# Attention keys turned with both parts at once, subtractions moved from GpSimd to VectorE, and modulation sums cut into other chunks

## The chip, the cores and the metric

One core of a Trainium2 chip runs the whole program. The metric is device microseconds from launch to end. The core has TensorE (matmuls, PE), VectorE (DVE), ScalarE (ACT), GpSimd (POOL) and SyncE (SP), which here only issues DMAs; GpSimd and ScalarE issue some too. Each engine runs its own instructions in the order fixed when the program was built.

## The reference, cut to what matters

Two layers over 512 latent and 256 context tokens of width 1024, in float32. Layer 0 has the Fourier and convolution mixer, layer 1 windowed attention with 16 query heads on 4 key heads of width 64. Every layer takes shift, scale and gate vectors from a modulation `silu(c) @ w_mod[layer] + b_mod[layer]` (six vectors of 1024), and ends in a mixture of experts behind a router:

```python
mod_l = (jax.nn.silu(c) @ w_mod[layer] + b_mod[layer])[:, None, :]
sh1_l, sc1_l, g1_l, sh2_l, sc2_l, g2_l = jnp.split(mod_l, 6, axis=-1)
hl = modulate(rms_norm(xl, norm_mix_g[layer]), sh1_l, sc1_l)
...
xl = xl + g1_l * yl
hl2 = modulate(rms_norm(xl, norm_ffn_g[layer]), sh2_l, sc2_l)
f = hier_moe(hl2, ...)     # router logits: hl2 @ w_router; 32 experts, top 2 of one group
```

In the attention, a score is the product of a normed and rotated query with a normed and rotated key, each 64 wide.

## The kernel before

Work is done in tiles of 128 tokens: `m` = 0 to 3 latent, 4 and 5 context. A float32 product that must be exact enough is made of two parts: an upper part `hi` (rounded to the type fp32r) and a lower part `lo = x - hi`, with three or four products of parts in place of one.

**The first mixer (lines 1200 to 1365, the functions `proj`, `four_a`, `four_b`).** Four Fourier groups `g` are followed by four convolution chunks `j`; each chunk makes three projections `proj` (48 matmuls each, L1259 and L1260), for which ScalarE writes `whi` (L1253) and VectorE `wlo` (L1255). Between them two other jobs are fed in small steps. `ModFeed.step` (`feed`) makes the modulation of layer 0 and the first third of layer 1's by matmuls (L1037) on 2 MB pieces of `w_mod`. `SumFeed.step` (`sums`) makes vectors 2 to 5 of layer 1's modulation on VectorE: 4 vectors of 8 steps, each step a multiply and add of a 128x1024 tile `mw` into `acc` (L1075). The tiles `mw`, 512 KB each, are loaded by DMAs that GpSimd issues (L1068); there are two buffers, and a load is issued when the step before last has left its buffer. After a vector's eighth step `finish` sums `acc` over the partitions by four matmuls (L1088), adds the bias on VectorE (L1090), and stores the vector to the DRAM table `mod_d` (L1091). The 32 steps lie three to a Fourier group (12) and five to a chunk (20); the last is at the very end of the last chunk.

**Where the sums lie in memory.** `acc` and `mw` are in the pool `sp`, which stands on the right-hand side beside `hp` (48 KB per partition, the mixer's inputs `hhi` and `hlo`). When the chunks are done, `cp, tp, sp, hp` are closed and the same place is given to `lst`, `x1p` (24 KB), `hq` (20 KB) and `rq`. In the program before, the tiles of `rq`, which are the router's weights `wr`, biases `br`, gains `gf`, the gate row `gr` and the router's modulation `md`, lie over `acc` and `mw`: `wr`, `br`, `gf` and the first `gr` over `acc`, `md` over a buffer of `mw`. A tile's load waits for the last user of the tiles under it.

**`mixer_out` (from line 1368).** It multiplies the mixer's output `ym` by `w_out` in two halves of the columns: per token tile 24 matmuls (L1436) into one of two PSUM tiles `A`, then VectorE multiplies by `gr` (L1440) and adds into `x1` (L1441). After the first tiles, `router` loads `md` (L1383) and makes 8 accumulated float32 matmuls on it, 16 in the trace (L1389). SyncE issues all of these loads. Then come routing, gathering, and the experts, whose weights SyncE streams through a ring of buffers (L723), each load waiting until TensorE has left its buffer.

**The attention's keys (lines 1680 to 1790).** `st_norm(m)` norms and turns a token tile into `hf` (one buffer), writes `hhi` on ScalarE (L1729) and `hlo` by a subtraction (L1733), on VectorE for `m` = 0 and on GpSimd for the other five. `st_kv(m)` projects keys and values (24 matmuls, L1715); `qk_norm_rope` norms and rotates the keys into `kk`, upper part in place 0 (L1704, ScalarE) and lower part in place 1 (L1705). `st_kt(m)` turns each part by four transposes of 128x64 (L1757) into a PSUM tile of 64 rows, which ScalarE copies to the rows 0 to 63 of `kS[part]` (L1758) and then VectorE to the rows 64 to 127 (L1759). A query column of `qS` has its upper part in rows 0 to 63 and its lower part below, so the two matmuls on `kS[0]` and `kS[1]` (L1833) give all four products.

The order within each engine is set by a planner that runs the program on its own clock and issues what is ready; `in_order` and `issue_after` pin some of it.

Of the kernel before, what the change touches and what calls it, by code (L numbers as in the profile page):

```python
# [10 lines left out]
F32 = mybir.dt.float32  # L11
F32R = mybir.dt.float32r
# [8 lines left out]
D = 1024  # L21
# [64 lines left out]
def body(tc, I, out, upto=None, dbg=None):  # L86
    nc = tc.nc
    V, S, G, T, Y = nc.vector, nc.scalar, nc.gpsimd, nc.tensor, nc.sync

    def pool(name, bufs=1, side="left", space=None):  # L90
        kw = dict(name=name, bufs=bufs, reuse_waits="tile")
        if space is None:
            kw["side"] = side
        else:
            kw["space"] = space
        g = tc.tile_pool(**kw)
        p = g.__enter__()
        p_close[id(p)] = g
        return p
# [39 lines left out]
    ident = K("ident")  # L139
# [907 lines left out]
    class SumFeed:  # L1047
# [1 line left out]


        def __init__(self, layer, vectors, room):
            self.layer, self.vectors, self.room = layer, vectors, room
            self.acc = room.tile([128, D], F32, name="acc")
            self.todo = [(v, k) for v in vectors for k in range(8)]
            self.w = []
            self.ld = 0
            for _ in range(2):
                self.load()

        def tile(self):  # L1060
            return self.room.tile([128, D], F32, name="mw", bufs=2)

        def load(self):
            if self.ld < len(self.todo):
# [5 lines left out]
        def step(self):  # L1070
            v, k = self.todo.pop(0)
            self.ld -= 1
            w = self.w.pop(0)
            if k:
                V.scalar_tensor_tensor(self.acc, w, sil[:, k, 0:1], self.acc, op0=ALU.mult, op1=ALU.add)  # L1075
            else:
                V.tensor_scalar(self.acc, w, sil[:, k, 0:1], None, op0=ALU.mult)
            if k == 7:
                self.finish(v)
            self.load()  # L1080

        def finish(self, v):

# [13 lines left out]
    def psA(shape):  # L1097
        return pp.tile(shape, F32, name="A", bufs=2)

    def psB(shape):  # L1100
        return pp.tile(shape, F32, name="B", bufs=3)
# [5 lines left out]
    st = pool("start")  # L1107
# [22 lines left out]
    for m in range(6):  # L1130
# [6 lines left out]
        dst, c0 = (xnl, m * 128) if m < 4 else (xnc, (m - 4) * 128)  # L1137
        for hf in range(2):
            p = psB([128, 4, 128])
# [28 lines left out]
    p = psA([64, 8, 128])  # L1168
# [6 lines left out]
    hhi = [hp.tile([128, 8, L], F32R, name="hhi0"), hp.tile([128, 8, LC], F32R, name="hhi1")]  # L1175
    hlo = [hp.tile([128, 8, L], F32R, name="hlo0"), hp.tile([128, 8, LC], F32R, name="hlo1")]
# [3 lines left out]
    mm = {}  # L1180
# [29 lines left out]
    sp = pool("sp", side="right")  # L1210
# [94 lines left out]
    prev = None  # L1305
    load_conv(0)
    pre = proj_pre()
    sums = SumFeed(1, (2, 3, 4, 5), sp)
    for g in range(4):
        aT = four_a(g)  # L1310
        if g:
            with tc.issue_after(mm["last"].ins):
                feed.step()
        sums.step()
        if prev is not None:
            four_b(g - 1, prev)
        feed.step()
        sums.step()
        sums.step()
        prev = aT  # L1320
    wo = I["w_out_even"][0].rearrange("(j p) d -> p j d", p=128)

# [7 lines left out]
    for j in range(4):  # L1330
        wr4 = wconv[j]
        pc = proj(lambda k0: wr4[:, k0:k0 + 4, 1, :])
        if prev is not None:
            four_b(3, prev)
            prev = None
            close(fp)
            cp = pool("cp")
            u = cp.tile([128, L + LC + 4], F32, name="ut")
            for c in (0, L + 1, L + 2, L + LC + 3):
                V.memset(u[:, c:c + 1], 0.0)  # L1340
        csb = tp.tile([128, L + LC + 4], F32, name="t3", bufs=2)
        S.copy(csb[:, 0:L + LC], pc)
        feed.step()
        sums.step()
        load_conv(j + 1)
        if j == 3:
            wout = load_wout(0, 1)
        phv = proj(lambda k0: wr4[:, k0:k0 + 4, 2, :])
        for o, p0, n in segs:
            V.tensor_mul(u[:, o:o + n], csb[:, p0:p0 + n], phv[:, p0:p0 + n])  # L1350
        z = cp.tile([128, L + LC + 4], F32, name="z", bufs=2)
        S.activation(z[:, 1:1 + N2], u[:, 1:1 + N2], AF.Copy, scale=cw[:, 1, j:j + 1])
        V.scalar_tensor_tensor(z[:, 1:1 + N2], u[:, 0:N2], cw[:, 0, j:j + 1], z[:, 1:1 + N2], op0=ALU.mult, op1=ALU.add)
        V.scalar_tensor_tensor(z[:, 1:1 + N2], u[:, 2:2 + N2], cw[:, 2, j:j + 1], z[:, 1:1 + N2], op0=ALU.mult, op1=ALU.add)
        feed.step()
        sums.step()
        sums.step()
        pb = proj(lambda k0: wr4[:, k0:k0 + 4, 0, :])
        for o, p0, n in segs:
            V.tensor_mul(z[:, o:o + n], z[:, o:o + n], pb[:, p0:p0 + n])  # L1360
        put_y(4 + j, [z[:, o:o + 256] for o in (1, 257, L + 3)])
        feed.step()
        sums.step()
        sums.step()
    close(cp, tp, sp, hp)


# [116 lines left out]
    x1p = pool("x1p", side="right")  # L1484
# [168 lines left out]
    cb = pool("cb")  # L1653
# [15 lines left out]
    hhi = [hpl.tile([128, 8, L], F32R, name="hhi")]  # L1669
    hlo = [hpl.tile([128, 8, L], F32R, name="hlo")]  # L1670

    kS = [kvp.tile([128, 4, L + LC], F32R, name=f"kS{i}") for i in range(2)]
# [8 lines left out]
    def qk_norm_rope(ps, nh, a, m, wk, rope, dst):  # L1681

        n = nh * 64
        sq = wk.tile([128, n], F32, name="sq")
        S.activation(sq, ps, AF.Square)
        ss = small.tile([128, nh], F32, name=f"ss{nh}")
        V.tensor_reduce(ss, sq.rearrange("p (h d) -> p h d", d=64), axis=AX.X, op=ALU.add)
        r = rstd_of(ss, nh, 64)
        o = wk.tile([128, n], F32, name="qo")
        ov = o.rearrange("p (h d) -> p h d", d=64)  # L1690
        pv = ps.rearrange("p (h d) -> p h d", d=64)
        if rope:
            V.tensor_mul(ov, pv, rot[:, a, m, 0, None, :].to_broadcast([128, nh, 64]))
            t = wk.tile([128, n], F32, name="sq")
            for h in range(2):
                def half(x, h):
                    return x.rearrange("p (n x h j) -> p n x h j", x=2, h=2, j=16)[:, :, :, h]
                sv = rot[:, a, m, 1, :].rearrange("p (x h j) -> p x h j", x=2, h=2)[:, :, h]
                V.tensor_mul(half(t, h), half(ps, 1 - h), sv[:, None].to_broadcast([128, nh, 2, 16]))
            G.tensor_add(o, o, t)  # L1700
        else:
            V.tensor_mul(ov, pv, gqk[:, a, None, :].to_broadcast([128, nh, 64]))
        V.tensor_mul(dst[:, :, 1], ov, r[:, :, None].to_broadcast([128, nh, 64]))
        S.copy(dst[:, :, 0].bitcast(F32R), dst[:, :, 1])  # L1704
        (G if nh == 8 and m < 2 else V).tensor_sub(dst[:, :, 1], dst[:, :, 1], dst[:, :, 0])  # L1705

    def toks(m):
# [10 lines left out]
    def st_norm(m):  # L1718
        if m < 2:
            hf_ = hfs[m]  # L1720
        else:
            xn = cb.tile([128, D], F32, name="xn", bufs=2)
            ss = small.tile([128, 1], F32, name="ss")
            S.activation(xn, x1[m], AF.Square, accum_out=ss)
            S.activation(xn, x1[m], AF.Copy, scale=rstd_of(ss, 1, D))
            hf_ = cb.tile([128, 8, 128], F32, name="hf")
            modulated(m, xn, hf_, psB)
        st, ms = toks(m)
        hi = S.copy(hhi[st][:, :, ms], hf_)  # L1729
        if m == 0:  # L1730

            tc.add_manual_dep(scaled[4].ins, hi.ins.name, mybir.DependencyInfo(mybir.DependencyClass.NoSync, mybir.DependencyReason.DATA), reason="order")
        (G if m else V).tensor_sub(hlo[st][:, :, ms], hf_, hhi[st][:, :, ms].bitcast(F32))  # L1733

    kro = {}
    late_kv = []

    def st_kv(m):
        ps = proj_qkv(m, [(wkv[0][0][:, k, :], wkv[0][1][:, k, :]) for k in range(8)], lambda a, b, c: (a, c, b) if m else (a, b, c))

        def after(wk):
            S.copy(vts[m], ps[:, 256:512])
            kk = cb.tile([128, 4, 2, 64], F32, name="kk", bufs=2) if m < 4 else x1p.tile([128, 8, 2, 64], F32, name=f"x{m}")[:, 0:4]
            qk_norm_rope(ps[:, 0:256], 4, 1, m, wk, m < 4, kk)
            kro[m] = kk

        if m < 5:
            after(cb)
        else:
            late_kv.append(after)  # L1750

    def st_kt(m):
        ms = slice(m * 128, (m + 1) * 128)
        for part in range(2):
            p = psB([64, 4, 128])
            for g in range(4):
                T.transpose(p[:, g, :], kro[m][:, g, part], ident)  # L1757
            S.copy(kS[part][0:64, :, ms], p)  # L1758
            (V.tensor_copy)(kS[part][64:128, :, ms], p)  # L1759

    raw0 = load_qkv(0, 3)
    for i in range(8):
# [251 lines left out]
```

## Time and profile before

| what | value |
|---|---|
| median of 3 runs | 1658.29 us (1654.82 to 1658.82) |
| the profiled execution | 1657.86 us, of it 1655.9 us span |
| TensorE busy, mean granted clock | 1525.1 us (92%), 0.965 |
| VectorE, ScalarE, GpSimd busy | 759.7, 440.3, 141.7 us |
| DMA | 503.50 MB, mean 304 GB/s |
| first mixer / its output and routing | up to 234 us / 234 to 360 us |
| experts of layer 0 / keys and queries / attention | to 860 / 860 to 980 / to 1100 us |

All times are microseconds from the span's start. The granted clock is a share of TensorE's full speed: 1.00 is its upper level (2.4 GHz), 0.50 its lower one (1.2 GHz). A row of waits names the engine and line that waited, and what ended the wait. The DMA share is that of the core's 16 DMA engines.

### The profile page before, as it was taken

The page shows a single profiled execution, that of the slowest core. Times are in us where ns is not written, and L with a number is a line of the kernel's source. Part 1 is how long each engine was busy: PE and PEld are TensorE (multiplying, and loading weights), DVE is VectorE, ACT ScalarE, POOL GpSimd, SP SyncE. Part 2 cuts the span into 40 slices and gives each one's busy share as a digit, 9 for nine tenths or more (in the row PEclk, how much of TensorE's full clock was granted, in tenths as well). Part 3 has the DMA queues.
Part 4 walks back from the last instruction along what each step waited for, and adds up shares of the span by engine and source line. Part 5 has one row for each costly group of instructions (what it writes and reads, how often), then busy time and mean ns, then how long its engine had stood idle before and what let it go on. Part 6 is the DMA issues. An engine that isn't in the chain of part 4 may idle for free.

```text
span 1655.9 us, 21500 instructions
## 1 busy us (share of the span) xinstructions
PE 1525.1 (92%) x8011; PEld 866.5 (52%) x8011; DVE 759.7 (46%) x1671; ACT 440.3 (27%) x879; POOL 141.7 (9%) x160
## 2 busy tenths in 40 slices
PE   4989997969999999999988989999799999997787
PEld 2757876843444434444447776668444544531332
DVE  4546553784342534333366975555622322320223
ACT  5322221311111111111046577644221222210110
POOL 2522100300000000000033210000000000000000
PEclk9999997979999999999979999999899999998999
DMA  9897672579999999999930121042699999999996
GB/s 387 306 389 246 229 245 82 189 278 424 425 424 424 381 394 424 425 424 424 407 121 1 51 52 52 1 128 76 237 426 427 426 426 427 426 416 427 426 427 260
DMA packets 108832, 503.50 MB, mean 304 GB/s; under 512 B 18784, under 2 KB 33632, under 8 KB 56752
## 3 DMA queue, kind: packets, MB, share of 16 engines
q1 hardware_dynamic: 93600, 447.31, 67.1%
q0 software_dynamic: 11952, 51.55, 8.2%
q10 hardware_dynamic: 3168, 3.17, 0.6%
q8 instruction: 66, 1.08, 0.3%
q14 instruction: 46, 0.38, 0.1%
HBM read 499.30 MB, written 5.32 MB: 305 GB/s over the span
## 4 chain that ended last, share of the span: by engine, by line
PE 34%; DMA 10%; DVE 3%; ACT 2%; issue 1%; SPq 0%; DVEq 0%; ACTq 0%
PE p L862 8%; PE yp L933 5%; DMA w<-in_w_dram 5%; DMA hhi<-in_w_dram 4%; PE A L1715 3%; PE cp L811 3%; PE A L1436 3%; PE tp L767 2%; PE A L1833 2%; PE O L1895 2%; PE B L1880 2%; ACT P L1839 1%; PE tp L774 1%; DVE x L812 1%; DMA w<-in_w_qkv_dram 0%
## 5 line engine op out<-in xcount | busy, mean ns | idle before, releaser
L862 PE MATMUL p<-w,xt 128*64 128x512 f32 (+1 forms) x1024 | 338.5, 611 | 14.3 <-DMA w<-in_w_dram 14.1
L862 PE MATMUL p<-r,xt 128*64 128x512 f32 (+1 forms) x784 | 284.2, 620 | 8.3 <-DMA r<-in_w_dram 7.9
L812 DVE TENSOR_TENSOR x<-x,cp 128x512 f32<-128x512 f32 x224 | 148.1, 685 | 96.5 <-PE cp L811 96.4
L875 DVE TENSOR_TENSOR sg<-sg,p 128x512 f32<-128x512 f32 x29 | 20.0, 688 | 365.9 <-PE p L862 354.9
L811 PE MATMUL cp<-y,ot 128*128 128x512 f32 x616 | 174.5, 419 | 8.3 <-DVE x L812 4.5
L862 PEld LDWEIGHTS p<-w,xt 128*64 128x64 f32 (+1 forms) x1024 | 99.6, 135 | 127.3 <-issue 98.6
L933 PE MATMUL yp<-w,ht 128*64 128x512 f32 (+1 forms) x512 | 158.7, 595 | 2.2 <-DMA w<-in_w_dram 2.2
L862 PEld LDWEIGHTS p<-r,xt 128*64 128x64 f32 (+1 forms) x784 | 84.5, 137 | 144.5 <-issue 124.8
L811 PEld LDWEIGHTS cp<-y,ot 128*128 128x128 f32 x616 | 107.2, 191 | 52.0 <-DVE x L812 26.3
L933 PE MATMUL yp<-r,ht 128*64 128x512 f32 (+1 forms) x368 | 128.7, 595 | 1.3 <-ACT ht L894 0.7
L799 ACT CAST y<-yp 128x512 fp32r<-128x512 f32 x58 | 34.0, 586 | 277.0 <-DVE yp L795 185.5
L1436 PE MATMUL A<-r,r 128*128 128x512 f32 x288 | 71.2, 404 | 2.2 <-ACT r L1402 1.4
L933 PEld LDWEIGHTS yp<-r,ht 128*64 128x64 f32 (+1 forms) x368 | 38.1, 134 | 66.7 <-issue 64.0
L862 PE MATMUL p<-hhi,xt 128*64 128x512 f32 (+1 forms) x128 | 66.0, 672 | 7.1 <-DMA hhi<-in_w_dram 7.1
L933 PEld LDWEIGHTS yp<-w,ht 128*64 128x64 f32 (+1 forms) x512 | 46.4, 131 | 45.6 <-issue 40.1
L1436 PEld LDWEIGHTS A<-r,r 128*128 128x128 f32 x288 | 55.1, 195 | 14.8 <-ACT r L1402 2.3
L1837 DVE CUSTOM_DVE_ANT_0 A<-A,band,nsink 128x640 f32<-128x640 f32 (+1 forms) x56 | 45.4, 831 | 35.4 <-PE A L1833 35.2
L865 ACT ACTIVATE sg<-p 128x512 f32<-128x512 f32 x29 | 17.3, 597 | 157.0 <-PE p L862 157.0
L801 DVE TENSOR_TENSOR y<-yp,y 128x512 fp32r<-128x512 f32 x58 | 40.1, 691 | 40.0 <-ACT y L799 40.0
L797 DVE SCALAR_TENSOR_TENSOR yp<-yp,gs,grow 128x512 f32<-128x512 f32 x26 | 19.7, 759 | 72.4 <-PE yp L933 72.4
L739 POOL DMA_INDIRECT r<-h_d,gi x17 | 17.0, 997 | 411.8 <-PE tp L774 342.4
L862 PE MATMUL p<-hlo,xt 128*64 128x512 f32 (+1 forms) x112 | 51.8, 611 | 0.0
(434 smaller groups left out, 2605.5 us busy)
## 6 DMA issues: line engine op xcount, KB each, us to landing
w<-in_w_dram SPq DMA_DIRECT2D x191, 1024.0 KB, 19.5
r<-in_w_dram SPq DMA_DIRECT2D x143, 1024.0 KB, 19.5
w<-in_w_mod_dram POOLq DMA_DIRECT2D x12, 2048.0 KB, 10.1
hhi<-in_w_dram SPq DMA_DIRECT2D x23, 1024.0 KB, 19.5
hlo<-in_w_dram SPq DMA_DIRECT2D x23, 1024.0 KB, 19.5
mw<-in_w_mod_dram POOLq DMA_DIRECT2D x32, 512.0 KB, 5.2
w<-in_w_in_even_dram SPq DMA_DIRECT2D x13, 512.0 KB, 11.2
w<-in_w_mod_dram SPq DMA_DIRECT2D x3, 2048.0 KB, 12.8
```

Source lines behind the costliest of these rows:

```text
L767: T.matmul(p, oh[:, m, :], near["h2"][m][i][:, hf * 512:hf * 512 + 512], start=n == 0, stop=n == 7)
L799: hi = S.copy(Yr[j, hf][0], ys)
L801: V.tensor_sub(Yr[j, hf][1], ys, Yr[j, hf][0].bitcast(F32))
L811: T.matmul(p, OT[j][:, m * 128:(m + 1) * 128], Yr[j, hf][i], start=n == 0 and i == 0, stop=n == len(js) - 1 and i == 1)
L812: return V.tensor_add(xs, xs, p)
L862: T.matmul(ps[rs], X[b][:, q, rs], W[j, wn, ab][:, q, :], start=q == 0, stop=q == 7)
L933: T.matmul(py_[hf][rs, :], HT[b][:, q % 4, rs], W[j, "w2", ab][:, q % 4, hf * 512:hf * 512 + 512], start=q % 4 == 0, stop=q % 4 == 3)
L1436: T.matmul(ps, lhs(m, a, j), whl[b][:, j, :], start=j == 0 and i == 0, stop=j == 7 and i == 2)
L1715: T.matmul(ps, h[st][:, k, ms], whl[k][b], start=k == 0 and i == 0, stop=k == 7 and i == 2)
L1833: T.matmul(ps[:, o0:o0 + w], qS[G_][:, c, b * 128:(b + 1) * 128], kS[part][:, 2 * G_ + c // 4, k0:k0 + w], start=part == 0, stop=part == 1)
L1837: V.tensor_tensor_reduce(out=ps[:, 0:w], in0=ps[:, 0:w], in1=bnd, op0=ALU.add, op1=ALU.min, scale=1.0, scalar=nsink[:, hd:hd + 1], accum_o ...
L1880: T.transpose(p[:, i, :], Ps[gl * 4 + i][:, t * 128:(t + 1) * 128], ident)
```

## The change

Three edits. In the first mixer the sums' object is made in the first Fourier group; the groups take 0, 1, 2 and 3 steps (6 in place of 12), and each chunk calls for 9 in place of 5 until none is left, so that steps lie in chunks 0, 1 and 2 (9, 9, 8) and none in chunk 3. From chunk 0 on, a second place for `mw` in the pool `cp` gives four buffers. In the attention, VectorE makes all `hlo`. A key tile `kk` gets three places (upper, lower, upper): ScalarE writes places 0 and 2 at once, and the transposes take places 0 and 1 together, then 1 and 2, so that one copy of 128 rows fills `kS[0]` (upper over lower) on ScalarE and one fills `kS[1]` (lower over upper) on VectorE.

```diff
 class SumFeed:
+        def more(self, *rooms):
+            self.rooms += rooms
             for _ in range(2):
                 self.load()
         def tile(self):
-            return self.room.tile([128, D], F32, name="mw", bufs=2)
+            self.at += 1
+            return self.rooms[self.at % len(self.rooms)].tile([128, D], F32, name="mw", bufs=2)
+        def steps(self, n):
+            for _ in range(min(n, len(self.todo))):
+                self.step()
...
-    sums = SumFeed(1, (2, 3, 4, 5), sp)
     for g in range(4):
-        sums.step()
+        if g == 0:
+            with tc.issue_after(mm["last"].ins):
+                sums = SumFeed(1, (2, 3, 4, 5), sp)
         if prev is not None:
             four_b(g - 1, prev)
         feed.step()
-        sums.step()
-        sums.step()
+        sums.steps(g)
...
             cp = pool("cp")
+            sums.more(cp)
...                                  # in a chunk j: 1, 2 and 2 steps before
-        sums.step()
+        sums.steps(3)
...
-        S.copy(dst[:, :, 0].bitcast(F32R), dst[:, :, 1])
+        S.copy(dst[:, :, 0::2].bitcast(F32R), dst[:, :, 1:2].to_broadcast([128, nh, dst.shape[2] - 1, 64]))
...
-        (G if m else V).tensor_sub(hlo[st][:, :, ms], hf_, hhi[st][:, :, ms].bitcast(F32))
+        V.tensor_sub(hlo[st][:, :, ms], hf_, hhi[st][:, :, ms].bitcast(F32))
...
-            kk = cb.tile([128, 4, 2, 64], F32, name="kk", bufs=2) if m < 4 else ...
+            kk = cb.tile([128, 4, 3, 64], F32, name="kk", bufs=2) if m < 4 else ...
...
-            p = psB([64, 4, 128])
+            p = psB([128, 4, 128])
             for g in range(4):
-                T.transpose(p[:, g, :], kro[m][:, g, part], ident)
-            S.copy(kS[part][0:64, :, ms], p)
-            (V.tensor_copy)(kS[part][64:128, :, ms], p)
+                T.transpose(p[:, g, :], kro[m][:, g, part:part + 2].rearrange("p a d -> p (a d)"), ident)
+            (V.tensor_copy if part else S.copy)(kS[part][:, :, ms], p)
```

## Rows read from the trace of the kernel before

**Rows 1.** Timeline of VectorE, then TensorE: start, length, instruction, [idle before <-ended by].
```profile
257.15 1.30 DVE L1440 TENSOR_TENSOR A<-A,gr 128x512 f32<-128x512 f32 x2 [14.90 <-DMA gr<-mod_d]
...
238.09 10.27 PE L1436 MATMUL A<-r,r 128*128 128x512 f32 x44 [0.83 <-DVE r L1403]
257.36 7.01 PE L1389 MATMUL B<-wr,md 128*128 128x36 f32 x32 [9.00 <-DMA md<-mod_d]
```

**Rows 2.** Timeline of SyncE's DMA issues, 233 to 257 us.
```profile
233.81 1.77 SPq L1490 DMA_DIRECT2D x<-in_x_dram  x4
...
242.28 0.33 SPq L723 DMA_DIRECT2D w<-in_w_dram  x1
242.71 0.56 SPq L1372 DMA_DIRECT2D wr<-in_w_router_g_dram  x1
...
244.07 8.57 SPq L1374 DMA_DIRECT2D br<-in_b_router_g_dram  x1
...
254.40 0.38 SPq L1383 DMA_DIRECT2D md<-mod_d  x1
```

**Rows 3.** Windows, L1436 alone: length, TensorE, its loads, then clock, DMA share, GB/s.
```profile
264.20:269.70 5.50, 5.50 (x13) 4.34 (x14) 0.50 0.00 0
269.70:283.00 13.30, 13.30 (x60) 10.96 (x60) 1.00 0.06 21
```

**Rows 4.** Chain of waits in layer 1, where the same router follows the mixer.
```profile
1106.52 1.71 PE B L1389 x16
```

**Rows 5.** Instructions on the tile acc, by line: ns, first and last start.
```profile
L1075 DVE SCALAR_TENSOR_TENSOR acc<-mw,sil,acc x28: 1274/1284/1286, 66.5 to 226.0; 128x1024 f32<-128x1024 f32 x28
```

**Rows 6.** Instructions on the tile mw; then L1068's times to landing.
```profile
L1090 DVE TENSOR_TENSOR mw<-B,mw x8: 671/680/683, 113.2 to 235.4; 1x512 f32<-1x512 f32 x8
...
DMA to landing us min/median/max: 3.8/5.2/12.6
```

**Rows 7.** Timeline of ScalarE: the first copy of the last two convolution chunks.
```profile
191.20 0.80 ACT L1342 COPY t<-A 128x768 f32<-128x768 f32 x1
...
217.35 0.80 ACT L1342 COPY t<-A 128x768 f32<-128x768 f32 x1
```

**Rows 8.** TensorE's waits, 60 to 240 us: total, times, longest.
```profile
PE M L1037 <- DMA w<-in_w_mod_dram: 3.4, 1, 3.4
```

**Rows 9.** Windows of the first mixer, all engines; the last three columns as above.
```profile
80.00:100.00 20.00, 20.00 (x137) 14.51 (x139) 10.54 (x20) 4.83 (x10) 4.26 (x7) 1.00 1.01 381
...
160.00:180.00 20.00, 20.00 (x121) 16.30 (x121) 11.64 (x14) 4.25 (x7) 3.86 (x7) 1.00 0.79 264
```

**Rows 10.** Groups by form, 860 to 936 us: busy us, mean ns, idle before.
```profile
L1759 DVE CAST kS<-B 64x512 fp32r<-64x512 f32 x12 | 7.9, 681 | 3.0 <-ACT kS L1758 2.8
...
L1733 POOL TENSOR_TENSOR w<-hf,w 128x1024 fp32r<-128x1024 f32 x2 | 4.8, 2408 | 10.4 <-DVE kS L1759 6.9 <-ACT w L1729 3.6
...
L1733 DVE TENSOR_TENSOR hlo<-r,hhi 128x1024 fp32r<-128x1024 f32 x1 | 1.2, 1226 | 0.5 <-ACT hhi L1729 0.5
```

**Rows 11.** Timeline of VectorE, two operations twice each, and of GpSimd.
```profile
897.12 1.50 DVE L1705 TENSOR_TENSOR kk<-kk 128x256 f32<-128x256 f32 x1
...
901.97 0.16 DVE L166 TENSOR_TENSOR rt<-rt,rv 128x4 f32<-128x4 f32 x1
...
903.44 0.41 DVE L1705 TENSOR_TENSOR kk<-kk 128x256 f32<-128x256 f32 x1
...
907.04 2.27 DVE L166 TENSOR_TENSOR rt<-rt,rv 128x4 f32<-128x4 f32 x1
...
906.86 2.42 POOL L1733 TENSOR_TENSOR w<-hf,w 128x1024 fp32r<-128x1024 f32 x1 [6.88 <-DVE kS L1759]
```

**Rows 12.** Chain of waits, where VectorE's run of small operations ends.
```profile
916.58 8.25 DMA w<-in_w_qkv_dram
```

**Rows 13.** TensorE's waits, 895 to 936 us.
```profile
PE B L1757 <- ACT hf L1614: 1.6, 1, 1.6
```

**Rows 14.** Windows, the experts of layer 0, all engines.
```profile
600.00:700.00 100.00, 99.81 (x469) 42.92 (x470) 40.66 (x66) 11.90 (x21) 2.97 (x3) 1.00 1.01 424
```

More of the change, by code (lines that the diff above doesn't have):

```diff
@@ L1051, in __init__ @@
         def __init__(self, layer, vectors, room):
-            self.layer, self.vectors, self.room = layer, vectors, room
+            self.layer, self.rooms, self.at = layer, [room], 0
             self.acc = room.tile([128, D], F32, name="acc")
@@ L1056, in __init__ @@
             self.ld = 0
+            self.more()
+        def more(self, *rooms):
+            self.rooms += rooms
             for _ in range(2):
@@ L1355, in body @@
         feed.step()
-        sums.step()
-        sums.step()
+        sums.steps(3)
         pb = proj(lambda k0: wr4[:, k0:k0 + 4, 0, :])
@@ L1362, in body @@
         feed.step()
-        sums.step()
-        sums.step()
+        sums.steps(3)
     close(cp, tp, sp, hp)
@@ L1742, in after @@
             S.copy(vts[m], ps[:, 256:512])
-            kk = cb.tile([128, 4, 2, 64], F32, name="kk", bufs=2) if m < 4 else x1p.tile([128, 8, 2, 64], F32, name=f"x{m}")[:, 0:4]
+            kk = cb.tile([128, 4, 3, 64], F32, name="kk", bufs=2) if m < 4 else x1p.tile([128, D], F32, name=f"x{m}")[:, 0:768].rearrange("p (h a d) -> p h a d", h=4, a=3)
             qk_norm_rope(ps[:, 0:256], 4, 1, m, wk, m < 4, kk)
```

## The prediction

> **What bounds the kernel now.** I read TensorE's waits first, then the timelines around the longest of them, then windows for the clock. In the convolution chunks TensorE has almost no gap, so edits beside it pay only where it waits. Its longest wait near the change comes right after the mixer: 9.0 us at line 1389, the router, for the DMA that brings `md` [rows 1]. Just before, VectorE stands 14.9 us for `gr` [rows 1]; without `gr` it can't free a PSUM tile, so TensorE has no other work after two token tiles. Both loads are late, and SyncE's issues show why [rows 2]: `x1` goes out at 233.81, `a`, `h` and `b` behind it, a 1 MB expert weight at 242.28, and only then `wr` at 242.71; the issue of `br` stands for 8.57 us behind these transfers, and `md` goes out at 254.40. The router's tiles lie over the sums' tiles, whose last use is the tail of the mixer, so the planner could not put their loads ahead of `x1`.
>
> The wait has a second price. After it TensorE's clock is granted at 0.50, its lower level, until 269.7: there 13 matmuls of L1436 take 5.50 us, 0.42 each, against 60 in 13.30 us, 0.22 each, at 1.00 [rows 3]. The router's 32 matmuls take 7.0 us [rows 1]; in layer 1, where its loads are in time, 16 take 1.71 us [rows 4], so 32 would take 3.4.
>
> **The change part by part.**
>
> *The sums end a chunk earlier.* All 32 steps stay, at 1.28 us each on VectorE [rows 5], and so do the four `finish`es. But the last of these, whose bias add stands at 235.4 us now [rows 6], moves into chunk 2. The first copies of chunks 2 and 3 stand at 191.2 and 217.35 [rows 7], so chunk 2 and the sums with it are over before 217, 16 us before `x1` is issued. Then `acc` and `mw` are free, and `wr`, `br`, `gf`, both `gr` and both `md` can be issued before `x1`, where SyncE has few loads. What they read of `mod_d` (layer 0) was written long before. So I take the whole wait: 9.0 us, plus the clock, 3.6 for the router (7.0 - 3.4) and 2.6 for L1436 (13 times 0.42 - 0.22): 15.2 us. Bounds: nothing if the order on SyncE stays; above, these 15.2. What is late next is `x1` for L1441: it goes out at 233.81 and is wanted when the first token tile's 24 matmuls are through, some 5 us (24 times 0.22) after their start near 236, so I see no new wait there, or a fraction of 1 us.
>
> *The tail.* VectorE's two bias adds (0.68 us each [rows 6]) now stand between the mixer's last product and the splitting of `w_out`, for which TensorE waits 0.8 us before 238 [rows 1]. Without them I take 0.8 us; between 0 and 1.4.
>
> *Fewer sums in the Fourier groups.* Six steps and their six 512 KB loads leave this stretch. TensorE waits there 3.4 us for a 2 MB piece of `w_mod` [rows 8], and the DMA engines are full (share 1.01, 381 GB/s) [rows 9]. About three of the loads would have gone out before the late piece, 1.6 MB, 4 us at that rate. I take 2.5 us; between 0 and 3.4.
>
> *More sums in the chunks.* Nine steps of 1.28 are 11.5 us in a chunk of 26.2 us [rows 5, 7], 5.1 more than now. VectorE has room: 11.6 us busy of 20 [rows 9], so some 15 or 16 of 20 then, beside a TensorE that is busy all the time; this hides them. What queues behind a step that waits for its tile is the next `wlo`, and TensorE behind that; three buffers of `wlo` are the cover. Eleven more loads in chunks 0 to 2, 5.8 MB in some 80 us, add 72 GB/s to 264 [rows 9], still under the 381 at which the engines were full. Cost between 0 and 4 us; I take 0.5 and set it against the 2.5 above: 2.0.
>
> *The keys.* VectorE loses six copies of 0.68 us (4.1), and ScalarE as many; the copies that remain have the same 512 columns, so I keep their length. VectorE gains five subtractions of 1.23 us (6.1) for which GpSimd took 2.4 each [rows 10]. ScalarE's rounding of a key tile doubles its 256 columns, which costs at most what the lost copy of 512 gives back. So on numbers VectorE loses 2.0 us. But while GpSimd subtracts, a small operation of VectorE that takes 0.16 us elsewhere took 2.27 and ended where GpSimd ended, and one of 0.41 took 1.50 [rows 11]: 3.2 us, so VectorE is 1.2 better off. The Trainium skill, SBUF — State Buffer, section "SBUF: two separate sides", calls the pair of ports that VectorE and GpSimd share an exclusive lock whose loser waits for the whole instruction; the trace agrees (2.27 beside a subtraction of 2.42). By the same rule a subtraction on VectorE, with two inputs in SBUF, holds up GpSimd's additions in the rotation, up to five times 1.2 us; no row shows that side, and if it fell on the chain the keys would bring nothing and the sum would be 3.0 less.
>
> How much of it counts? VectorE's run of small operations sets when the load of the queries' second weights goes out, at 916.58 [rows 12]. From 896 on this run loses three copies (2.0), the two blocked spells (3.2) and part of the 2.8 us in which VectorE waited for ScalarE's half of a copy [rows 10], and gains two subtractions (2.5): some 3 us or more. TensorE's own waits in that stretch, which cap the gain, are five of 4.1 us in all, the longest 1.6 [rows 13]. I take 3.0; between -2 (the extra work on VectorE, nothing freed) and 5. The transposes keep their number and their 128 columns: nothing.
>
> **What passes to the end.** In the experts of layer 0 TensorE is busy 99.8 of 100 us and the DMA share is 1.01 [rows 14]. Both are full, so nothing there absorbs a gain, and SyncE's loads wait for buffers that TensorE frees, those of the mixer's output among the first; so they shift with it.
>
> **The sum**, on the profiled execution (1657.9 us, 0.4 below the median): 15.2 + 0.8 + 2.0 + 3.0 = 21.0, so 1636.9, or 1637.3 against the median. I write 1637.
>
> **Rivals.**
>
> *The order stays* (10%): SyncE still issues the router's loads behind `x1`, `a`, `h`, `b` and the expert weight. For it: SyncE's order is a plan's, and the 8.57 us of `br` are a queue, not a wait for the sums. Against: that plan does not keep the program's order, as `a`, `h` and `b` come later in it than `wr`, so it goes by what is free. Then 0.8 + 2.0 + 3.0 = 5.8 remain: 1652.
>
> *The gap closes, but the experts give the time back* (8%): their weights or the gathers would start at a time that the mixer does not set. For it: the DMA engines are full in the experts. Against: their buffers are freed by TensorE. Then the keys' 3.0 and little else: 1655.
>
> *Slower: the chunks starve on `mw`* (7%). 26 steps in some 80 us ask for a tile every 3.1 us. A load lands in 5.2 us in the median, 12.6 at the worst [rows 6]; with the step of 1.28 behind it, four buffers give a tile every 1.6 us, at the worst 3.5. VectorE runs in order, so a late tile holds the next `wlo`, and TensorE with it. It decides from a landing of 11.1 us on ((11.1 + 1.3) / 4 = 3.1). At 14 us the steps take 26 x 3.8 = 99, which eats the gain; at 16 us 26 x 4.3 = 112, 32 more than there is: 1669. For it: 12.6 was seen where the DMA engines were full. Against: they have room in the chunks.
>
> **How the numbers follow.** The forecast has 75%, the rivals 10, 8 and 7. The forecast's own range is 1630 (the upper bounds, 15.2 + 1.4 + 3.4 + 5 = 25.0, and 2 for a new order elsewhere) to 1648. With the first rival in, 8 times in 10: 1629 to 1653. A measurement of this kernel tells about 0.3%, 5 us, from no change: faster are the forecast and most of the first rival, 0.82; same 0.11; slower 0.07.
>
> **What would show it.** Right: `wr`, `gr` and `md` issued before the mixer's last matmul; no wait of TensorE at L1389; clock 1.00 from 236 to 283; the sums' last store before 217; five more of L1733 on VectorE at 1.23, and no small operation of 2 us there. Wrong: `wr` still behind a weight load; waits at L1259 for `wlo` in chunks 0 to 2; VectorE waiting over 20 us for `mw`; GpSimd's additions late in the keys.

## The result

The changed kernel took 1642.89 us in the median of 6 runs (1641.75 to 1646.03), the kernel before 1657.07 in 6 runs beside it (1654.22 to 1661.06). The ratio is 0.9916 [0.9899, 0.9933]: 14 us faster. The forecast was 1637, 6 us less: of its gain of 21 us, 14 came. Measured once more, in another group of runs (after_again), the ratio was 0.9913 [0.9899, 0.9928].

The profiled execution took 1642.09 us, its span is 1640.0, so 15.9 us less span than before. Lines of the changed kernel are numbered up to 10 higher. Cutting both spans at the same five events of TensorE's timeline shows where the time went. The events are the start of the first 256-column projection in the Fourier groups, the end of the last one of the chunks, the end of the last output matmul of the first mixer, and the starts of the first key projection and of the first product with the values:

| stage, us | before | after | change | forecast |
|---|---|---|---|---|
| start | 71.98 | 73.00 | +1.0 | 0 |
| Fourier groups and chunks | 161.74 | 156.73 | -5.0 | -2.0 |
| mixer's output and router | 100.16 | 89.13 | -11.0 | -16.0 |
| routing and experts of layer 0 | 529.30 | 529.49 | +0.2 | 0 |
| keys and queries | 122.43 | 121.24 | -1.2 | -3.0 |
| rest | 670.31 | 670.43 | +0.1 | 0 |

How firm each line is shows in second profiles of the same two kernels (both stand with the experiments). Before gave 72.08, 163.29, 99.31, 528.65, 122.24 and 669.28; after 71.94, 156.72, 90.13, 527.47, 119.68 and 670.59. So the start's +1.0 is a matter of the single execution, and the experts move by 2 us on their own. The 1.6 us between the two profiles of the changed kernel in keys and queries are the clock: TensorE is idle for 9.4 and 9.5 us there, and the granted clock is 0.94 and 0.96. The 1.5 us between those of the kernel before in groups and chunks go with 3.4 us at 0.50 in the second one (106.4 to 109.8).

**The mixer's output.** SyncE's issues after answer to [rows 2]:

```profile
229.81 1.77 SPq L1499 DMA_DIRECT2D x<-in_x_dram  x4
...
232.71 0.56 SPq L1381 DMA_DIRECT2D wr<-in_w_router_g_dram  x1
233.31 3.14 SPq L1382 DMA_DIRECT2D wr<-in_w_router_e_dram  x1
236.49 3.25 SPq L1383 DMA_DIRECT2D br<-in_b_router_g_dram  x1
...
241.40 0.38 SPq L1392 DMA_DIRECT2D md<-mod_d  x1
...
242.81 0.46 SPq L1404 DMA_DIRECT2D a<-mod_d  x1
...
246.58 10.66 SPq L723 DMA_DIRECT2D w<-in_w_dram  x2
```

The router's loads moved ahead of `a`, `h`, `b` and the expert weight, but not ahead of `x1`. Measured from the issue of `x1`, `md` goes out after 11.6 us (241.40 - 229.81); before it was 20.6. TensorE's timeline shows what is left of the gap, as start, length and [idle before, ended by]:

```profile
232.08 11.18 PE L1445 MATMUL A<-r,r 128*128 128x512 f32 x48 [2.35 <-ACT r L1411]
245.46 1.97 PE L1398 MATMUL B<-wr,md 128*128 128x36 f32 x16 [2.20 <-DMA md<-mod_d]
248.35 12.75 PE L1445 MATMUL A<-r,r 128*128 128x512 f32 x48 [0.92 <-DVE x L1450]
260.94 1.87 PE L1398 MATMUL B<-wr,md 128*128 128x36 f32 x16
```

The 9.0 us [rows 1] became 2.2, and a wait of 0.9 for `x1` came behind it. Windows of the output matmuls alone, first before, then after, with the granted clock as third number from the end:

```profile
252.60:269.70 17.10, 5.52 (x13) 4.43 (x14) 0.50 0.45 126
```

```profile
248.30:251.70 3.40, 3.35 (x8) 2.67 (x9) 0.50 1.02 405
251.70:270.00 18.30, 16.76 (x74) 13.55 (x73) 1.00 0.39 146
```

The stretch at the lower level is 3.4 us instead of 17.1. The second profile of the kernel before has 7.0 us of wait for `md` and 13.7 us at 0.50 that begin in it, with 3.4 us more at 0.50 earlier in the output matmuls; that of the changed kernel has 1.4 + 1.1 us of waits and twice 3.4 us at 0.50.

**Fourier groups.** Before, TensorE's list had two more waits between 60 and 120 us beside the 3.4 us for `w_mod` [rows 8]:

```profile
PE A L1299 <- DVE Z L1287: 1.5, 1, 1.5
PE B L1088 <- DVE acc L1075: 0.8, 1, 0.8
```

That is 5.7 us together. After, between 60 and 235 us, the list has only the 2.4 us at the mixer's end. VectorE's waits for `mw` in the same stretch are down to two rows:

```profile
DVE acc L1083 <- DMA mw<-in_w_mod_dram: 1.6, 1, 1.6
DVE acc L1081 <- DMA mw<-in_w_mod_dram: 1.5, 2, 1.2
```

**Keys.** The five subtractions are on VectorE at the forecast length, and the copies keep theirs. GpSimd's busy time falls from 141.7 to 129.6 us, VectorE's from 759.7 to 752.8. Groups by form, 840 to 925 us (busy, mean ns, idle before); the first form is one of three with two each:

```profile
L1742 DVE TENSOR_TENSOR hlo<-hf,hhi 128x1024 fp32r<-128x1024 f32 x2 | 2.5, 1225 | 0.7 <-ACT hhi L1738 0.7
...
L1767 DVE CAST kS<-B 128x512 fp32r<-128x512 f32 x6 | 4.1, 685 | 3.9 <-PE B L1766 3.9
```

The load of the queries' second weights, in the chain of waits:

```profile
899.58 8.36 DMA w<-in_w_qkv_dram
```

It goes out 51.2 us after the first key projection; before it was 53.4 [rows 12]. But behind it TensorE has a wait for VectorE that the kernel before did not have:

```profile
923.21 2.10 PE L1724 MATMUL A<-w,hhi 128*128 128x512 f32 x6 [2.67 <-DVE rq L168]
```

### The profile page after: what moved, and what is told of

Same layout as the page of the kernel before. It is cut to its first block, busy times and chain, and to the rows that moved or that the text cites. A ratio compares the mean times of both kernels' runs of the same rounds, so it can differ in the third digit from the quotient of the medians.

```text
span 1640.0 us, 21488 instructions
## 1 busy us (share of the span) xinstructions
PE 1521.7 (93%) x8011; PEld 864.6 (53%) x8011; DVE 752.8 (46%) x1670; ACT 438.5 (27%) x873; POOL 129.6 (8%) x155
## 4 chain that ended last, share of the span: by engine, by line
PE 34%; DMA 10%; DVE 3%; ACT 2%; issue 1%; SPq 0%; ACTq 0%; DVEq 0%
PE p L862 8%; PE yp L933 5%; DMA w<-in_w_dram 5%; DMA hhi<-in_w_dram 4%; PE A L1724 3%; PE cp L811 3%; PE A L1445 3%; PE A L1841 2%; PE tp L767 2%; PE O L1903 2%; PE B L1888 2%; ACT P L1847 1%; PE tp L774 1%; DMA w<-in_w_qkv_dram 1%; DVE x L812 1%
## 5 line engine op out<-in xcount | busy, mean ns | idle before, releaser
L862 PE MATMUL p<-w,xt 128*64 128x512 f32 (+1 forms) x1024 | 332.9, 605 | 12.9 <-DMA w<-in_w_dram 12.7
L862 PE MATMUL p<-hhi,xt 128*64 128x512 f32 (+1 forms) x128 | 61.4, 632 | 5.9 <-DMA hhi<-in_w_dram 5.9
L1445 PEld LDWEIGHTS A<-r,r 128*128 128x128 f32 x288 | 54.4, 192 | 14.6 <-ACT r L1411 2.7
L779 ACT COPY xt<-tp 128x512 f32<-128x512 f32 x34 | 18.4, 589 | 118.3 <-PE tp L774 118.2
## 6 DMA issues: line engine op xcount, KB each, us to landing
w<-in_w_in_even_dram SPq DMA_DIRECT2D x13, 512.0 KB, 15.9
w<-in_w_mod_dram SPq DMA_DIRECT2D x3, 2048.0 KB, 11.6
```

The lines of the kernel that those rows point to most:

```text
L862: T.matmul(ps[rs], X[b][:, q, rs], W[j, wn, ab][:, q, :], start=q == 0, stop=q == 7)
L1445: T.matmul(ps, lhs(m, a, j), whl[b][:, j, :], start=j == 0 and i == 0, stop=j == 7 and i == 2)
```

## The experiments

The theory: 11 us come from SyncE's order, which is set by where the last sum ends; 5 from the Fourier groups; the keys bring about 1. Ratios are against the kernel before, beside each kernel on its chip; that kernel's medians were 1655.04, 1655.22 and 1654.52 us in three groups of four. The stages of the table above, by profile:

| kernel | start | groups, chunks | output, router | experts | keys, queries | rest |
|---|---|---|---|---|---|---|
| sums_only | 71.96 | 156.73 | 90.69 | 528.38 | 117.59 | 670.64 |
| keys_hlo | 71.91 | 161.53 | 98.38 | 529.60 | 118.64 | 670.44 |
| hlo_only | 72.75 | 163.23 | 97.98 | 528.90 | 120.44 | 669.67 |
| sums_late | 72.71 | 155.53 | 98.48 | 531.14 | 119.58 | 670.91 |
| sums_early_two | 72.37 | 163.17 | 91.77 | 527.69 | 116.82 | 669.76 |
| router_gpsimd | 73.20 | 156.73 | 84.02 | 529.17 | 121.10 | 671.14 |
| sq_two | 71.86 | 156.72 | 91.41 | 529.59 | 122.22 | 669.10 |
| splits_in_order | 73.48 | 156.72 | 89.36 | 529.53 | 122.68 | 670.67 |
| best_keys | 72.98 | 156.72 | 84.06 | 528.99 | 121.02 | 669.58 |
| best_sums | 72.05 | 156.73 | 85.61 | 529.78 | 117.19 | 669.97 |

**The parts by themselves: sums_only, keys_hlo, hlo_only.** The first is the changed kernel with these lines set back:

```diff
-        V.tensor_sub(hlo[st][:, :, ms], hf_, hhi[st][:, :, ms].bitcast(F32))
+        (G if m else V).tensor_sub(hlo[st][:, :, ms], hf_, hhi[st][:, :, ms].bitcast(F32))
...
+            p = psB([64, 4, 128])        # and the copies, kk and its rounding as before
```

The second is the kernel before with these two edits made, the third with the first alone.

> The sums' part of the change alone; keys and lower parts as before. Theory: of the 14 to 16 us gained, 11 come after the mixer (SyncE takes the router's loads ahead of a, h, b and a weight, because acc and mw are free) and 4 to 5 in the Fourier groups and chunks (VectorE's waits for mw fall from 25 us to 3), 1 is lost at the start, and the keys bring 1. Then this kernel gains 13 to 15: 1643 to 1645, with the first output matmul of the mixer 4 us earlier and the last 15 us earlier than before. Rival, the keys carry their predicted 3 or more: 1646 or above, and the stretch from the experts' end to the first score is no shorter than before.

> The keys' part and the lower parts on VectorE alone; the sums as before. Theory: the keys' projections end 2.5 to 3 us earlier, then TensorE waits some 2.5 us for VectorE in the queries, so 1 us is left at the scores: 1655.5 to 1657. Rival of the prediction: 3 us are left, 1654. Second rival, these edits bring more without the sums' new start: over 5 us, 1652 or less. Nothing changes before 850 us by more than 1 us in any of them.

> Only the lower parts of the keys' inputs move from GpSimd to VectorE; keys turned as before. If the port that both engines share is what held the keys, the small operation of 2.27 us goes, and the first query transposes come 2 us or more earlier, as in the whole change (2.9). If the six copies less are what shortened the stretch, these transposes come within 0.7 us of before, or later, since VectorE has five subtractions of 1.2 us more. Time at the end: 1655 to 1658 either way.

Measured: sums_only 1638.64 us, 0.9905 [0.9891, 0.9920]; keys_hlo 1651.61, 0.9978 [0.9969, 0.9988]; hlo_only 1653.36, 0.9991 [0.9982, 1.0000]. By itself the sums' part gives all of the gain, 16.4 us, a little over the theory's 13 to 15. The keys' part alone gives 3.4, as the prediction had it and about 2 more than the theory here allowed. The two don't add: 16.4 + 3.4 stands against 14 measured for the whole. The table says why. With the old keys code, keys and queries take 122.4 us before but 117.6 in sums_only, where no line of that stage was edited; with the new code they take 121.2 and 119.7. In that stage of before and of sums_only (windows of all TensorE work, clock third from the end) TensorE is busy as long and at the same mean clock, but idle for 11.0 and 6.2 us:

```profile
863.18:985.61 122.43, 111.48 (x568) 0.96 0.13 35
```

```profile
847.75:965.34 117.59, 111.35 (x568) 0.96 0.14 37
```

The new code's kernels have the one long wait; first keys_hlo, then sums_only, whose list from 895 to 985 us has no row over 1.1:

```profile
PE A L1715 <- DVE rq L168: 2.7, 1, 2.7
```

```profile
PE B L1803 <- ACT P L1848: 1.1, 1, 1.1
PE A L1842 <- DVE sq L1708: 1.0, 1, 1.0
```

In hlo_only the first query transposes come 68.3 us after the first key projection, as before (68.4), and in keys_hlo after 64.1. So the removal of GpSimd's subtractions moved nothing up to there; that gain came with the new transposes and the six copies less, as far as two different plans can be compared. Behind that point hlo_only is about 2 us shorter than before (its stage is 120.44); its order there is another too, so which of the two brought this isn't shown.

**Where the last sum ends: sums_late and sums_early_two.** The first is the changed kernel, the second the kernel before:

```diff
# sums_late, at the three places of a chunk
-        sums.steps(3)
+        sums.steps(2)                     # the last two: 3 if j == 3 else 2
# sums_early_two, at the three places of a chunk (before: 1, 2 and 2)
+        sums.steps(3)
```

> The whole change, but with 2 sums at a place in the chunks instead of 3, and 3 at the last two, so that the last sum is again at the mixer's end; the groups' 0, 1, 2, 3 and the four buffers stay. Theory (where the last sum ends sets SyncE's order): a, h, b and a weight go out ahead of wr again, TensorE waits 8 to 9 us for md at the router and runs some 17 us at the lower clock; of the gain 4 to 6 remain: 1651 to 1654. Rival (the gain comes from fewer sums in the Fourier groups and from more buffers): 1643 to 1645 as with the whole change.

> The kernel before (its Fourier groups with three sums each, its two buffers, its keys) with one edit: three sums at each place of the chunks instead of 1, 2 and 2, so that the last sum ends in the third chunk. Theory (where the last sum ends sets SyncE's order): wr goes out ahead of a, h, b and the weight, the wait for md falls from 9.0 to some 2 us and the stretch at the lower clock from 17 us to some 3: 9 to 11 us gained, 1644 to 1647, with nothing gained by the Fourier groups. Rival (two buffers starve the denser sums): VectorE's waits for mw grow above their 25 us, wlo comes late and TensorE waits at the projections of chunks 0 to 2; up to 10 us are lost there and 1650 or more is left.

Measured: sums_late 1648.97 us, 0.9963 [0.9950, 0.9976]; sums_early_two 1643.72, 0.9929 [0.9916, 0.9943]. Of sums_late's gain of 6 us, 4 to 6 were expected. SyncE's order in it is that of before, and so, nearly, is the wait, with 13.7 us at 0.50 where 17 were expected:

```profile
231.20 0.38 SPq L1404 DMA_DIRECT2D a<-mod_d  x1
...
236.61 0.33 SPq L723 DMA_DIRECT2D w<-in_w_dram  x1
237.04 0.56 SPq L1381 DMA_DIRECT2D wr<-in_w_router_g_dram  x1
...
248.20 0.38 SPq L1392 DMA_DIRECT2D md<-mod_d  x1
```

```profile
PE B L1398 <- DMA md<-mod_d: 8.5, 1, 8.5
```

Its groups and chunks take 155.53 us. So most of that gain belongs to the lighter groups. The 1.2 us more of the changed kernel (156.73 - 155.53) are not a price of its denser chunks: TensorE waits for nothing in that stage in either kernel. They are mostly the last `finish`, four matmuls that stand ahead of the last projections in the changed kernel and behind them, in the next stage, in sums_late (first the changed kernel, then sums_late):

```profile
214.61 1.05 PE L1098 MATMUL B<-acc,onef 128*32 128x512 f32 x4
```

```profile
228.17 1.05 PE L1098 MATMUL B<-acc,onef 128*32 128x512 f32 x4
```

The rival, that groups and buffers carry all of it, falls. In sums_early_two the order is the new one (`wr` at 238.54, right behind `x1`, and `a` only at 249.45) and the router's wait falls to 3.1 us with two buffers, while the Fourier wait stays (TensorE's waits, then VectorE's):

```profile
PE M L1037 <- DMA w<-in_w_mod_dram: 3.8, 1, 3.8
PE B L1391 <- DMA md<-mod_d: 3.1, 1, 3.1
...
DVE acc L1075 <- DMA mw<-in_w_mod_dram: 18.3, 12, 4.7
```

Its output stage is 91.77, that is 7.5 to 8.4 us under before; VectorE's waits for `mw` were 18.3 + 3.1 us, where the same list of before has 20.9 + 4.0, and its 163.17 in groups and chunks lies between the two profiles of before. The starving rival falls even with two buffers. Its keys and queries took 116.82, again with no edit there, so the whole gains 12 us where 9 to 11 were expected.

**What is left of the gap: router_gpsimd.** The changed kernel with five loads and `md` of layer 0 on another queue:

```diff
+        Q = Y if layer else G
-        Y.dma_start(wr[:, :, 0:4], I["w_router_g"][layer].rearrange("(p k) e -> p k e", k=8))
+        Q.dma_start(wr[:, :, 0:4], I["w_router_g"][layer].rearrange("(p k) e -> p k e", k=8))
...                                  # the same for the rest of wr, br, gf and md
```

> The changed kernel with the loads of layer 0's router (wr, br, gf, md) issued by GpSimd, which stands idle there, so that they no longer queue behind x1 on SyncE. If SyncE's order is what is left of the gap, wr goes out at about 230 instead of 232.7, md before 236 instead of 241.4, the wait of 2.2 us for md, the 0.9 us behind it and the 3.4 us at the lower clock go: 3 to 4 us less than the changed kernel. Rival: the many small pieces of wr, not the queue, are slow, or x1 is late next: 0 to 1 us less.

Measured: 1636.10 us, 0.9881 [0.9864, 0.9897]; 5 us under the changed kernel's 1641.20 on the same chip, where 3 to 4 were expected. GpSimd's issues, then TensorE's timeline, then a window of 51 us (all engines; clock third from the end):

```profile
218.12 0.94 POOL L1382 DMA_DIRECT2D wr<-in_w_router_g_dram  x1
219.05 0.91 POOL L1383 DMA_DIRECT2D wr<-in_w_router_e_dram  x1
219.96 0.56 POOL L1384 DMA_DIRECT2D br<-in_b_router_g_dram  x1
...
221.58 1.45 POOL L1393 DMA_DIRECT2D md<-mod_d  x2
```

```profile
232.29 19.14 PE L1446 MATMUL A<-r,r 128*128 128x512 f32 x83 [2.35 <-ACT r L1412]
251.27 1.87 PE L1399 MATMUL B<-wr,md 128*128 128x36 f32 x16
```

```profile
232.00:283.00 51.00, 50.71 (x251) 42.90 (x252) 28.54 (x48) 11.78 (x22) 2.98 (x2) 1.00 0.47 166
```

`wr` goes out at 218.12, where about 230 was expected, 12 us ahead of `x1`: its place was free as soon as the sums were done, as the prediction said, and only the planner's place for it on SyncE held it back. The stage takes 84.02 us, 16.1 under before and 15.3 under its second profile; the prediction's 15.2 + 0.8 is 16.0.

**The keys' give-back: after_again, sq_two, splits_in_order.** The changed kernel, unchanged, and with one edit each:

```diff
# sq_two
-        sq = wk.tile([128, n], F32, name="sq")
+        sq = wk.tile([128, n], F32, name="sq", bufs=1 if wk is cb else 2)   # and the rotation's t
# splits_in_order
...                                  # the second weights' splits are taken out of m == 0
+        with in_order(*([mybir.EngineType.DVE] if (G_, m) == (0, 1) else [])):
+            if (G_, m) == (0, 1):
+                wq[1] = split_to(load_qkv(512, 3), slot(1, ...), slot(2, ...), V)
             qk_norm_rope(ps, 8, 0, m, qp, True, qq)
```

> The changed kernel once more, beside the next three on one chip, so that a few us can be told apart: 14 to 16 us under the kernel before. For the keys: the 2.7 us wait of TensorE for VectorE in the queries stands in this kernel, in the keys' part alone and in the variant with late sums, and in none of the three kernels without the new transposes; it should stand here again, within 0.2 us.

> The changed kernel with two buffers instead of one for the tile of squares in the queries, which the rotation uses a second time. Theory: the new 2.7 us wait comes from that one buffer: ScalarE's square of a query tile waits until GpSimd has added the rotation of the tile before (idle of 1.0 and 3.2 us, put down to GpSimd), and VectorE frees the PSUM tile late. Then the wait and the clock's fall behind it go: 2.5 to 4 us less than the changed kernel. Rival: VectorE is late by its own order, the splits of the second weights among the rotations; then the wait stays and the time is within 1 us of the changed kernel's.

> The changed kernel, with VectorE's eight splits of the second query weights put in one run ahead of the second query tile's rotation, as the planner has them in the kernels without the new transposes. Theory (VectorE's order makes the new 2.7 us wait: four splits stand between the rotations, beside GpSimd's additions): the wait goes, and the queries end 3 to 4 us earlier against the keys' start; 1637 to 1639 where the changed kernel has 1641. Rival (the new transposes and copies themselves delay the queries): the wait stays above 2 us and the time within 1 us of the changed kernel's.

Measured: after_again 1641.20 us, 0.9913 [0.9899, 0.9928], the wait there again (2.5); sq_two 1642.89, 0.9925 [0.9912, 0.9939]; splits_in_order 1643.57, 0.9927 [0.9913, 0.9940]. Neither edit helped. With two buffers ScalarE's squares no longer wait for GpSimd, but TensorE's wait stays, 2.9 us; with the splits in one run it stands at another query tile, 3.2 us. First sq_two, then splits_in_order (VectorE's run of splits, then TensorE):

```profile
924.49 3.20 PE L1724 MATMUL A<-w,hhi 128*128 128x512 f32 x8 [2.94 <-DVE rt L166]
```

```profile
910.02 5.33 DVE L1548 TENSOR_TENSOR w<-w,w 128x512 fp32r<-128x512 f32 x7
...
918.74 3.75 PE L1724 MATMUL A<-P,hhi 128*128 128x512 f32 x8 [3.21 <-DVE sq L1708]
```

Both theories of that wait fall as they were put, though each edit also changed VectorE's order elsewhere in the stage. What makes the whole wait stays open; the account of the keys below shows a part of it.

**Both mends, and the kernel before once more: best_keys, best_sums, before_again.** best_keys is the changed kernel with the edits of router_gpsimd and splits_in_order; best_sums is sums_only with that of router_gpsimd; before_again is unchanged.

> Both mends together: the changed kernel with the router's loads of layer 0 issued by GpSimd (5 us less in its own run) and the splits in one run (3 to 4 us by the theory). They lie in different stages, so they should add: 1632 to 1634. If the splits' order is not the cause: 1636, as with the router's loads alone.

> The sums' part with the router's loads on GpSimd, keys and lower parts as in the kernel before. By the theory that the keys' part brings nothing by itself: 1633 to 1634, that is 5 us under the sums' part alone. If the keys' part is worth its predicted 3 us once its wait is gone, this kernel is 2 to 3 us above the one with both mends.

> The kernel before once more, with its profile, for the spread of its stages: time within 0.2% of its other runs. If the planner's order alone makes the keys and queries long in it, the stretch from the first key projection to the first product with the values takes 122 us again (117 and 118 us in the two kernels that have the same code there and the sums ended early). If that stretch is a matter of the single execution, it comes out at 117 to 120 us here.

Measured: best_keys 1635.93 us, 0.9888 [0.9873, 0.9904], no better than router_gpsimd; best_sums 1632.77, 0.9865 [0.9850, 0.9880], the fastest of all, 8 us under the changed kernel by the ratios. Its output stage is 85.61, 1.6 longer than that of router_gpsimd, behind the same wait of 2.35 us and with the same 83 matmuls, because TensorE's clock was granted at 0.50 from 232.4 to 235.8:

```profile
231.13 20.74 PE L1446 MATMUL A<-r,r 128*128 128x512 f32 x83 [2.35 <-ACT r L1412]
```

For the keys, before_again took 1654.94, 1.0001 [0.9992, 1.0010], with 122.2 us in keys and queries again. So that length goes with the kernel, not with the single execution.

## Why the forecast was right, and where it was not

**The router's gap: mechanism right, size 5 us too large.** The step that failed is "Then `acc` and `mw` are free, and `wr`, `br`, `gf`, both `gr` and both `md` can be issued before `x1`". They could: router_gpsimd issued those of the router there, and its stage lost 16.1 us (14.6 in best_sums, where the clock fell once). On SyncE the planner still took `x1` first, which waits for the last projection, so `md` came 9.0 us earlier against `x1` and not 20. That leaves 2.2 + 0.9 us of waits and 3.4 us at the lower clock. I had the rival for it, "the order stays", as all or nothing; it came half. sums_late shows that the end of the sums alone decides the order, and that the clock has a price of its own is borne out: the wait and most of its slow stretch left together.

**The tail: a near number by luck.** From the last projection to the end of the first 48 output matmuls it was 14.6 us before (248.36 - 233.72) and is 13.5 after, 1.1 less where I had 0.8. But TensorE's waits there did not fall: 1.4 + 0.8 us before, 2.35 after. TensorE now waits for ScalarE's half of that splitting instead of VectorE's. The 1.1 are about the four matmuls of the last `finish` (1.05 us), which moved ahead of the last projections and cost the same there. So this term, the wait for VectorE behind its bias adds, brought nothing by itself.

**Groups and chunks: 2.0 forecast, 5.0 measured.** I took 2.5 of the one wait of 3.4 [rows 8]. All three waits went, 5.7 us: with six fewer loads ahead of the late piece VectorE's `acc` and `Z` were in time too. (The first loads also start later, and no run parts the two; the extra buffers come only behind these groups, and sums_early_two, with the old groups, keeps the waits.) Of the 5.7, about 1 us went to the last `finish`, now inside this stage. The denser chunks, for which I had 0.5, cost TensorE no wait. VectorE and the DMAs covered them as argued. The starving rival was to decide from a landing of 11.1 us on; a load of `mw` now takes 6.7 us in the median and 11.6 at worst, but a single slow one costs VectorE 1.6 us of waiting, and TensorE nothing. I had priced the worst landing as if it were every one.

**The keys: 3.0 forecast, 1.2 and 2.7 in the two profiles of the whole change, 3.6 alone.** The load of the second weights did go out earlier against the first key projection (51.2 us for 53.4), but by less than 3, and the queries gave 2.7 us back in a new wait. Half of the reasoning was wrong, and the sum for the part alone came near by luck: the blocked spells, 3.2 us in my account, brought nothing up to the first query transposes in hlo_only; the new transposes and copies together did. The spells themselves are real, and several remain after. One stands in the new wait of TensorE, which ends when VectorE has read the old PSUM tile for the last time (VectorE's two rows, then GpSimd's):

```profile
921.69 1.04 DVE L166 TENSOR_TENSOR rt<-rt,rv 128x8 f32<-128x8 f32 x1
922.65 0.41 DVE L1708 TENSOR_TENSOR sq<-A,rot 128x256 f32<-128x256 f32 x1
...
921.44 1.26 POOL L1714 TENSOR_TENSOR x<-x 128x512 f32<-128x512 f32 x1 [5.01 <-ACT x L1713]
```

An operation that takes 0.16 us in the median here ends with GpSimd's subtraction. The Trainium skill, SBUF — State Buffer, section "SBUF: two separate sides", has the loser of that shared port wait for the whole instruction; this row agrees. The last read, L1708, stands right behind it and TensorE starts 0.15 us after that read, so some 0.9 of the 2.7 us are this spell, an estimate from these rows (1.04 - 0.16). The waits in keys_hlo, after_again and sq_two have the same spell in the same place; that in splits_in_order has none, but VectorE's 5.33 us of splits. Here, then, spells were worth nothing up to the first query transposes, and 0.9 us where VectorE was what TensorE waited for. The other side, additions of GpSimd held up by VectorE's subtractions for 1.2 us each, didn't come: the longest addition took 1.61 us, and 1.33 before.

**The signs named beforehand.** Right: five more subtractions on VectorE, no small operation of 2 us. Nearly: the sums' last store stands at 217.4, and 217 was named. Half: `md` is late by 2.2 us, and the clock's fall is short. Wrong: `wr`, `gr` and `md` were to be issued before the mixer's last matmul. None of the signs against the mechanism came: no wait of the chunks' projections for `wlo`, 3.1 us of waiting for `mw` instead of 20, and no addition of GpSimd held up by a whole subtraction.

**What passes to the end:** right. The experts took 529.3 and 529.5 us, so the gain ahead of them arrived whole.

**The total:** the time lies in the range that was given, but the terms do not all bear it out: 5 us too much at the router and 2 at the keys, against 3 too little in the Fourier groups. That these partly cancel is luck.

**What I did not see** is that the planner can lay out keys and queries anew for an edit elsewhere. From the same source there, the traces of sums_only and of the kernel before have TensorE's, VectorE's and ScalarE's instructions of that stage in different orders; it took 122.4 and 122.2 us in the kernel before, 116.8 to 117.6 in sums_only, sums_early_two and best_sums, whose orders are almost the same. Not every edit does this: with the new keys code the order is the same whether the sums end early or late (after and sums_late, 119.6 to 121.2 us). Beside the early sums the new keys code is no gain: by stage it costs 2 to 4 us (119.7 to 121.2), by the ratios 1 to 3 (0.9913 for 0.9905, and 0.9881 for 0.9865 with the router's loads on GpSimd). The ratios of sums_only and the changed kernel overlap; the runs of best_sums (1631.27 to 1633.13) and of best_keys (1634.28 to 1637.63) do not, though best_keys differs in the splits too. Why the early sums bring the old code that better order, and whether the new keys could have one as good, wasn't settled.

## What to carry to other kernels

When a freed buffer lets a load go earlier, ask which queue will issue it and what the planner puts in front of it: here 5 of 16 us lay in that queue, and an idle engine's queue brought them. Gains of parts measured alone need not add where a planner orders the engines; compare the stages that no edit touched as well. A late load costs the wait and the slow clock behind it, so price both, and from more than one profile: the same short wait cost 1.6 us of clock in one kernel and none in another.

## What the runs showed of the hardware

The same issue of `br`, 4 values for each partition, stood for 8.57 us on SyncE behind an expert weight [rows 2], for 3.25 ahead of it, and for 0.56 on GpSimd's queue at 219.96, ahead of `x1` as well. Waits of 9.0, 8.5 (sums_late) and 7.0 us (before_again) went with 17.1, 13.7 and 13.7 us at 0.50, which began in the wait; two waits of 2.2 and 0.9 us with a short router between them went with 3.4 us. A wait of 2.35 us at the mixer's end, the same in nine profiles, was followed by no fall in five of them (in router_gpsimd the clock stayed at 1.00 for 51 us) and by 3.4 us at 0.50 in four (after_again, sums_only, sq_two and best_sums). What decides between the two isn't shown here; between router_gpsimd and best_sums it was worth 1.6 us.

An operation of VectorE that takes 0.16 us stood for 1.04 beside a subtraction of GpSimd, and the matmuls that waited for VectorE started 0.9 us later by the rows; five subtractions taken from GpSimd moved the first query transposes by 0.1 us (hlo_only).
